# Gated networks: a fourth room for raw up weights, the fourth block's parts in an unread quarter of x

## Chip, cores and metric

The kernel runs on one core of a Trainium2 chip. A core has five engines that work side by side and wait for each other through semaphores: PE (TensorE: matmuls; PEld is its weight load), DVE (VectorE), ACT (ScalarE), POOL (GpSimd) and SP (SyncE, which here only issues DMAs). The metric is the device time of one execution in microseconds.

## The reference

Two residual layers over 512 tokens with 1024 channels. The first mixes tokens by a grouped state-space model, the second by attention with forget gates; each is followed by a gated network, which is what this change is about.

```python
def conv_ffn(h, w_up, conv_w, conv_b, w_down):
    up = h @ w_up                      # 1024 -> 2 * 2816
    a, b = jnp.split(up, 2, axis=-1)
    ...                                # a_conv: causal depthwise conv (width 3) of a
    return (jax.nn.silu(a_conv) * b) @ w_down

for i in range(DEPTH):                 # DEPTH = 2
    shift, scale, gate = adaln_params(c, ada_w[i, 0], ada_b[i, 0])
    hn = modulate(h, norm_g[i, 0], shift, scale)
    m = s5_mixer(...) if i % 2 == 0 else fox_mixer(...)
    h = h + gate * m
    shift, scale, gate = adaln_params(c, ada_w[i, 1], ada_b[i, 1])
    hn = modulate(h, norm_g[i, 1], shift, scale)
    h = h + gate * conv_ffn(hn, ffn_w_up[i], ffn_conv_w[i], ffn_conv_b[i], ffn_w_down[i])
return rmsnorm(h, final_g)
```

## The kernel before

Everything is float32. For PE a value is split into two rounded parts, `hi` (ACT, L303) and `lo` = value - `hi` (DVE, L304), by `put_parts`; a product of two such values is three matmuls, `hi*hi`, `hi*lo` and `lo*hi`. Activations lie with channels on the 128 partitions and tokens in the free dimension. The normed input of a gated network is `x`, a pair of tiles `a_hi` and `a_lo`, each of 8 blocks of 128 channels by 512 tokens.

**Pairs.** The 44 output blocks of `w_up` come as 22 pairs, f = 0 to 21: block 2f belongs to `a` of the reference, block 2f + 1 to `b`. A block is 128 rows by 1024 inputs, loaded as one raw tile of 512 KB. Pairs 0 to 3 of each layer are computed plainly (`product`, L320, 24 matmuls of 512 columns for a block). Pairs 4 to 21 go through `quarters`, which takes the two blocks of a pair, cut in two along the inputs, and `x`, cut in two along inputs and along tokens, as 2 by 2 block matrices, and forms their product from seven block products (L588) instead of eight. Each of the seven is 12 matmuls of 256 columns. Four kinds of weights are made for a pair:

- `a11`, `a12`: the two halves of the first block `a`, rounded as they are (1024 columns);
- `s1`, `s2` (tile c) and `s4`, `s3` (tile d): sums of quarters, four DVE instructions of L556 (`sums`), and then rounded (2 x 1024 columns);
- `a22`: the second half of the second block `b`, rounded as it is (512 columns).

On the other side stand quarters of `x` and four sums of quarters, `t1` to `t4`, which `forms_x` makes once a layer, during the plain pairs. The seven products are `a11*b11`, `s1*t1`, `a12*b21`, `s2*t2`, `s4*b22`, `a22*t4`, `s3*t3`. They read the quarters b11, b21 and b22 of `x` (first inputs and first tokens, second inputs and first tokens, second inputs and second tokens); none reads the fourth quarter, b12 (first four blocks of channels, tokens 256 to 511). ACT copies some products out of PSUM (L595, `nm_h`), DVE adds them up (L556, `nm_t`), and `gated` does the convolution (L638, L640), the gate (L643, L650) and the rounding of the result `g` (`ghi`, `glo`). Between pairs the blocks of the down product of the group before (`w_down`, L320, result added to `h` at L402) are computed.

**Rooms.** A raw block stays in its room until ACT and DVE have read it. The tag `raw` has three rooms (`RAW` in the second line quoted below), through which nearly all raw weights go in turn: the two blocks of each pair, and in the second layer also the pieces of `w_down`, which in the first layer have two rooms of their own (`rawd`, L194). The raw blocks of a pair are both loaded with `self.raw` at the head of `quarters`. SP issues these loads in the order in which the program has them and waits, at each, until the room is free. The rounded parts of `a22` have one room of their own in the network's pool, `w_hi` of 640 and `w_lo` of 544 columns; those of all others come from five rooms each.

**Order.** A scheduler at build time puts each engine's instructions in a fixed order, by its own estimate of when each would be ready; at run time an engine takes them strictly in that order. In the first layer DVE has additional work up to pair 16: 24 reductions (`ada_units`, L273) that make the modulation of the next layers, on blocks that POOL loads into the single room `ada_raw`.

Of the kernel before, what the change touches and what calls it, by code (L numbers as in the profile page):

```python
# [9 lines left out]
F32 = mybir.dt.float32  # L10
F32R = mybir.dt.float32r
# [7 lines left out]
P = 128  # L19
D = 1024  # L20
KT = D // P
# [46 lines left out]
ROOM, ASIDE, VALUES = 9 * P, 22, 16  # L68
# [7 lines left out]
def part_of(pool, shape, name, tag, bufs, aside=0):  # L76

    _, n, w = shape
    t = pool.tile([P, ROOM if bufs == WB else n * w + P], F32R, name=name, tag=tag, bufs=bufs)
    return t[:, aside:aside + n * w].rearrange("p (n w) -> p n w", w=w)  # L80


class Trunk:
# [464 lines left out]
    def quarters(self, pool, l, f, x, finish):  # L548

        nc = self.nc  # L550
        H, N = KT // 2, S // 2
        t1, t2 = HALVES
        a, b = (self.raw([P, KT, P], self.io["w_up"][l][2 * f + j]) for j in range(2))
        a11, a12, a21, a22 = a[:, :H], a[:, H:], b[:, :H], b[:, H:]
        c, d = (pool.tile([P, 2, H, P], F32, name="sums", bufs=2) for _ in range(2))
        sub = lambda o, u, v, op=ALU.subtract: nc.vector.tensor_tensor(o, u, v, op)  # L556
        w = {}
        copied = self.copied

        def parts(src, names, *where):  # L560
            hi, lo = (
                pool.tile([P, H * P + (P if n == "w_hi" else 32)], F32R, name=n, tag="e" + n)[:, ASIDE:ASIDE + H * P].rearrange("p (n w) -> p n w", w=P)
                if where else part_of(self.wpool, [P, len(names) * H, P], n, n, WB, ASIDE)
                for n in ("w_hi", "w_lo")
            )
            with self.behind(*copied):
                self.put_parts(hi, lo, src)
            for j, n in enumerate(names):
                w[n] = hi[:, j * H:(j + 1) * H], lo[:, j * H:(j + 1) * H]

        parts(a, ("a11", "a12"))
        sub(c[:, 0], a21, a22, ALU.add)
        sub(c[:, 1], c[:, 0], a11)
        parts(c.rearrange("p n k m -> p (n k) m"), ("s1", "s2"))
        sub(d[:, 1], a11, a21)
        sub(d[:, 0], a12, c[:, 1])
        parts(d.rearrange("p n k m -> p (n k) m"), ("s4", "s3"))
        parts(a22, ("a22",), pool)
        quarter = lambda k, t: tuple(v[:, k * H:(k + 1) * H, t] for v in x)
        xs = {"b11": quarter(0, t1), "b21": quarter(1, t1), "b22": quarter(1, t2)}  # L580
        for n, v in self.tx.items():
            xs[f"t{n}"] = v

        def times(o, wn, xn, first=True):
            (whi, wlo), (xhi, xlo) = w[wn], xs[xn]
            for k in range(H):
                for n, (wt, xt) in enumerate(((whi, xhi), (whi, xlo), (wlo, xhi))):
                    self.last_mm = nc.tensor.matmul(  # L588
                        o, wt[:, k], xt[:, k], start=(first and k == 0 and n == 0), stop=(k == H - 1 and n == 2),
                        skip_group_check=True,  # L590
                    )

        def copy(o, last=False):
            t = self.tmp.tile([P, N], F32, name="nm_h", bufs=4)
            a = nc.scalar.activation(t, o, AF.Copy)  # L595
            if last:
                self.copied = [a.ins]
            return t

        p1, p5 = (self.mm.tile([P, S], F32, name="mmp")[:, :N] for _ in range(2))  # L600
        p2, p4 = (self.aux.tile([P, S], F32, name="aux")[:, :N] for _ in range(2))
        oa, ob = (self.tmp.tile([P, S], F32, name="nm_t") for _ in range(2))
        times(p1, "a11", "b11")
        c1 = copy(p1)
        times(p5, "s1", "t1")
        c5 = copy(p5)
        times(p2, "a12", "b21")
        sub(oa[:, t1], p2, c1, ALU.add)
        times(p1, "s2", "t2", False)
        c2 = copy(p1, True)  # L610
        times(p5, "s4", "b22", False)
        sub(oa[:, t2], p5, c2, ALU.add)
        finish(2 * f, oa, slice(0, S))
        times(p4, "a22", "t4")
        c4 = copy(p4)
        times(p1, "s3", "t3", False)
        sub(ob[:, t2], p1, c5, ALU.add)
        sub(ob[:, t1], p1, c4)
        finish(2 * f + 1, ob, slice(0, S))
# [98 lines left out]
class Ew:  # L718
# [29 lines left out]
    def sub(self, a, b, out=None):  # L748
        return self.tt(a, b, ALU.subtract, out)
# [1147 lines left out]
```

## Time and profile before

| | |
|---|---|
| timed runs, median of 3 | 1200.07 us (1199.22 to 1203.46) |
| profiled execution | 1197.47 us, span of its trace 1195.7 us |
| mean granted clock of PE | 0.996 |
| bytes read from HBM, and their rate | 173.73 MB, 151 GB/s over the span |
| plain pairs and pair products of the first layer | up to 565 us; first pair product at 296.35 us |
| pair products of the second layer | 890 to 1149 us |
| SP waiting to load raw blocks until DVE has rounded a block (L304) | 468.4 us in 128 waits |
| SP waiting for the same until DVE has formed sums (L556) | 166.0 us in 18 waits |

How to read the rows below. A row of the page's first part gives an engine's busy time, its share of the span and its instructions. In the view by stages each row is a stretch of time (microseconds from the span's start) with its length, the busy time of each engine, the granted clock of PE and what the DMA engines did. A row of waits reads: engine, what it was to write, its line, `<-` who released it: total, number, longest. A row in order of time has the start, the duration, the engine, the line, the operation, `out<-in`, the shape, and in brackets how long the engine had been idle and what ended that. A row with `min/median/max` gives the durations in nanoseconds of all instructions of one kind.

### The profile page before, as it was taken

Reading aid. Unit: us, or ns where it says so; the run is one execution under the profiler, and the core shown is the slowest. Engines: PE = TensorE matmul, PEld = TensorE weight load, DVE = VectorE, ACT = ScalarE, POOL = GpSimd, SP = SyncE. Lnnn points to the kernel's source line nnn. Section 1 sums busy time; section 2 is a strip of 40 time slices with the busy share of each in tenths; the row PEclk is TensorE's granted clock in tenths of the full one; section 3 lists DMA queues with packets and bytes.
Section 4 is the critical chain, followed back from the end, with each engine's and each line's share of the span. In section 5 each row is a group of like instructions: output and inputs, shape, how many; then the busy total and the mean of one; then the engine's idle time right before and its main releaser. Section 6 shows DMA issues by size and latency. Waiting matters only on the chain.

```text
span 1195.7 us, 20776 instructions
## 1 busy us (share of the span) xinstructions
PE 1174.6 (98%) x7983; PEld 1021.7 (85%) x7983; DVE 1011.1 (85%) x1836; ACT 619.9 (52%) x1186; POOL 124.1 (10%) x230
## 2 busy tenths in 40 slices
PE   9999999999999899999999999999999999999997
PEld 4566678898999889999998788878989999999987
DVE  8989887889999989998786678867899887888865
ACT  3564644436554445455452566564456555545543
POOL 3231012100000000000000444330000000000000
PEclk9999999999999999999999999999999999999999
DMA  9588777721554445332454444433122342323331
GB/s 371 202 330 275 214 249 274 271 73 53 177 176 133 168 167 185 133 102 87 151 175 165 139 150 157 139 111 106 56 88 80 124 136 76 110 90 110 111 101 72
DMA packets 72115, 182.02 MB, mean 152 GB/s; under 512 B 23135, under 2 KB 25023, under 8 KB 70991
## 3 DMA queue, kind: packets, MB, share of 16 engines
q1 hardware_dynamic: 58767, 136.77, 34.5%
q0 software_dynamic: 11920, 43.26, 10.1%
q8 instruction: 63, 1.03, 0.3%
q10 hardware_dynamic: 1328, 0.66, 0.2%
q14 instruction: 37, 0.30, 0.1%
HBM read 173.73 MB, written 6.92 MB: 151 GB/s over the span
## 4 chain that ended last, share of the span: by engine, by line
PE 58%; issue 19%; DVE 12%; DMA 7%; ACT 1%; POOL 1%; SPq 0%; DVEq 0%; POOLq 0%; ACTq 0%
PE mmp L320 24%; PE mmp L588 12%; PE aux L588 5%; PE mmp L1277 4%; DVE w_lo L304 3%; DMA raw<-in_w_up 3%; PE mmp L1617 2%; PE aux L1035 1%; PE aux L1756 1%; PE mmp L229 1%; DVE sums L556 1%; PE aux L1776 1%; PE aux L1147 1%; DVE h L402 1%; DVE conv L640 1%
## 5 line engine op out<-in xcount | busy, mean ns | idle before, releaser
L304 DVE TENSOR_TENSOR w_lo<-raw,w_hi 128x1024 fp32r<-128x1024 f32 (+4 forms) x173 | 181.0, 1050 | 29.8 <-ACT w_hi L303 29.4
L303 ACT ACTIVATE w_hi<-raw 128x1024 fp32r<-128x1024 f32 (+4 forms) x173 | 154.0, 898 | 97.3 <-PE mmp L320 40.2
L320 PE MATMUL mmp<-ghi,w_hi 128*128 128x512 f32 (+1 forms) x412 | 147.5, 358 | 0.0
L320 PE MATMUL mmp<-glo,w_hi 128*128 128x512 f32 (+1 forms) x412 | 147.3, 358 | 0.0
L320 PE MATMUL mmp<-ghi,w_lo 128*128 128x512 f32 (+1 forms) x412 | 146.8, 356 | 0.0
L588 PE MATMUL mmp<-w_hi,w_lo 128*128 128x256 f32 x432 | 120.1, 278 | 3.3 <-DVE w_lo L304 3.3
L588 PE MATMUL mmp<-w_hi 128*128 128x256 f32 x432 | 120.1, 278 | 1.0 <-ACT nm_h L595 1.0
L588 PE MATMUL mmp<-w_lo,w_hi 128*128 128x256 f32 x432 | 119.7, 277 | 0.0
L320 PE MATMUL mmp<-a_hi,w_hi 128*128 128x512 f32 (+1 forms) x304 | 109.7, 364 | 0.0
L320 PE MATMUL mmp<-a_hi,w_lo 128*128 128x512 f32 (+1 forms) x304 | 107.9, 355 | 0.0
L320 PE MATMUL mmp<-a_lo,w_hi 128*128 128x512 f32 (+1 forms) x304 | 107.8, 356 | 0.0
L303 ACT ACTIVATE w_hi<-sums 128x1024 fp32r<-128x1024 f32 x80 | 83.9, 1058 | 44.3 <-DVE sums L556 38.9
L304 DVE TENSOR_TENSOR w_lo<-sums,w_hi 128x1024 fp32r<-128x1024 f32 x80 | 97.6, 1219 | 0.6 <-ACT w_hi L303 0.6
L595 ACT ACTIVATE nm_h<-mmp 128x256 f32<-128x256 f32 x108 | 40.3, 379 | 100.8 <-PE mmp L588 100.5
L320 PEld LDWEIGHTS mmp<-ghi,w_lo 128*128 128x128 f32 x412 | 77.4, 188 | 11.7
L320 PEld LDWEIGHTS mmp<-ghi,w_hi 128*128 128x128 f32 x412 | 77.3, 188 | 10.6
L320 PEld LDWEIGHTS mmp<-glo,w_hi 128*128 128x128 f32 x412 | 77.4, 188 | 10.2
L588 PEld LDWEIGHTS mmp<-w_hi,w_lo 128*128 128x128 f32 x432 | 81.5, 189 | 3.7 <-DVE w_lo L304 3.7
L588 PEld LDWEIGHTS mmp<-w_hi 128*128 128x128 f32 x432 | 81.7, 189 | 1.5 <-ACT nm_h L595 1.4
L588 PEld LDWEIGHTS mmp<-w_lo,w_hi 128*128 128x128 f32 x432 | 81.6, 189 | 0.0
L588 PE MATMUL mmp<-a_hi,w_lo 128*128 128x256 f32 x288 | 80.1, 278 | 0.8 <-DVE w_lo L304 0.8
L588 PE MATMUL mmp<-a_hi,w_hi 128*128 128x256 f32 x288 | 80.2, 278 | 0.6 <-ACT w_hi L303 0.6
(337 smaller groups left out, 3138.7 us busy)
## 6 DMA issues: line engine op xcount, KB each, us to landing
raw<-in_w_up SPq DMA_DIRECT2D x88, 512.0 KB, 3.7
ada_raw<-in_ada_t POOLq DMA_DIRECT2D x40, 512.0 KB, 4.1
raw<-in_ada_w POOLq DMA_DIRECT2D x24, 512.0 KB, 7.2
nf<-nfd SPq DMA_DIRECT2D x8, 1152.0 KB, 7.8
raw<-in_ada_w SPq DMA_DIRECT2D x16, 512.0 KB, 10.0
raw<-in_fox_qk SPq DMA_DIRECT2D x16, 512.0 KB, 3.6
raw<-in_w_down SPq DMA_DIRECT2D x24, 320.0 KB, 2.9
rawd<-in_w_down SPq DMA_DIRECT2D x24, 256.0 KB, 3.9
```

What stands on the lines that cost most here:

```text
L229: self.last_mm = nc.tensor.matmul(ps[32 * qq:32 * qq + 32, :], self.sc32[:, k, :], w[:, q * S:(q + 1) * S], start=(step is steps[0]), stop ...
L303: self.rounded = nc.scalar.activation(hi, src, AF.Copy).ins
L304: return nc.vector.tensor_tensor(lo, src, hi.bitcast(F32), ALU.subtract)
L320: self.last_mm = self.nc.tensor.matmul(o if len(xt.shape) == 2 else by_place(o), wt, xt, start=(k == 0 and n == 0), stop=(k == nk - 1 and ...
L402: add = self.nc.vector.scalar_tensor_tensor(h, ps, self.par[i][:, 16 + m:17 + m], h, op0=ALU.mult, op1=ALU.add,)
L556: sub = lambda o, u, v, op=ALU.subtract: nc.vector.tensor_tensor(o, u, v, op)
L588: self.last_mm = nc.tensor.matmul(o, wt[:, k], xt[:, k], start=(first and k == 0 and n == 0), stop=(k == H - 1 and n == 2), skip_group_che ...
L595: a = nc.scalar.activation(t, o, AF.Copy)
L640: c = nc.vector.scalar_tensor_tensor(t[:, d:], ps[:, :S - d], cw[:, 2 - d, f:f + 1], t[:, d:], op0=ALU.mult, op1=ALU.add)
L1035: nc.tensor.matmul(ps[:, :, cols], x[:, q, r].rearrange("p c j -> p (c j)"), both[:, :, planes, q, :], start=(r == 0), stop=(r == 1), skip ...
L1277: one = lambda k: nc.tensor.matmul(ps, w[m][:, k, :], x[:, k], start=(k == 0), stop=(k == KT - 1))
L1617: self.last_mm = nc.tensor.matmul(ps[q, b][:, :n], xt[:, k, tb], wt, start=(k == 0 and i == 0), stop=(k == KT - 1 and i == 2),)
```

## The change

Two things. The second block of a pair with an odd f is loaded into a new tile, `rawx`, with one room in the network's pool; a pair with an even f loads both blocks through `raw` as before. And the rounded parts of `a22` no longer have a room of their own: they are written into the quarter b12 of `a_hi` and `a_lo`, four runs of 128 columns, each in the second half of one of the first four blocks of channels. The old room held 640 + 544 columns of 4 bytes; `rawx` holds 1024.

```diff
-        a, b = (self.raw([P, KT, P], self.io["w_up"][l][2 * f + j]) for j in range(2))
+        a = self.raw([P, KT, P], self.io["w_up"][l][2 * f])
+        if f % 2:
+            b = pool.tile([P, KT, P], F32, name="rawx", bufs=1)
+            nc.sync.dma_start(b, self.io["w_up"][l][2 * f + 1])
+        else:
+            b = self.raw([P, KT, P], self.io["w_up"][l][2 * f + 1])
...
-        def parts(src, names, *where):
+        def parts(src, names, where=None):
             hi, lo = (
-                pool.tile([P, H * P + (P if n == "w_hi" else 32)], F32R, name=n, tag="e" + n)[:, ASIDE:ASIDE + H * P].rearrange("p (n w) -> p n w", w=P)
+                where[i][:, :H, N + ASIDE:N + ASIDE + P]
                 if where else part_of(self.wpool, [P, len(names) * H, P], n, n, WB, ASIDE)
-                for n in ("w_hi", "w_lo")
+                for i, n in enumerate(("w_hi", "w_lo"))
             )
...
-        parts(a22, ("a22",), pool)
+        parts(a22, ("a22",), x)
```

Lines behind the edit count five higher in the changed kernel: L556 becomes L561, L588 becomes L593. Only the pair products' surroundings are put in another order; POOL's order is the same, and of PE's matmuls 159 change places, all in pairs 10 to 14 of the first layer.

On SP, the first layer's loads from the last plain pairs to pair 9, before:

```order
L194 DMA rawd<-in_w_down 128x512 x2
L197 DMA raw<-in_w_up 128x1024 x7
L194 DMA rawd<-in_w_down 128x512 x2
L197 DMA raw<-in_w_up 128x1024 x2
L194 DMA rawd<-in_w_down 128x512 x2
```

And now, in the same place:

```order
L194 DMA rawd<-in_w_down 128x512 x2
L556 DMA rawx<-in_w_up 128x1024
L197 DMA raw<-in_w_up 128x1024 x7
L194 DMA rawd<-in_w_down 128x512 x2
L197 DMA raw<-in_w_up 128x1024
L556 DMA rawx<-in_w_up 128x1024
L194 DMA rawd<-in_w_down 128x512 x2
```

Pair 5's second block now stands ahead of all loads that wait for a room of `raw`, and each odd pair's is a load of its own.

On DVE, from the convolution of pair 12 to the rounding of pair 13's tile c (`w_lo<-sums`, the weights of `s1` and `s2`), before:

```order
L650 TENSOR_TENSOR conv<-conv,nm_t 128x512
L280 TENSOR_TENSOR par_94<-ada_s,rest 128x8
L402 SCALAR_TENSOR_TENSOR h<-mmp,par_93,h 128x512
L282 SCALAR_TENSOR_TENSOR ga_98<-par_94,rest 128x8
L304 TENSOR_TENSOR glo<-conv,ghi 128x512
L402 SCALAR_TENSOR_TENSOR h<-mmp,par_93,h 128x512
L304 TENSOR_TENSOR w_lo<-sums,w_hi 128x1024
L273 ISA ada_raw,ada_s<-ada_raw,c_row 128x1024
```

And now:

```order
L280 TENSOR_TENSOR par_94<-ada_s,rest 128x8
L402 SCALAR_TENSOR_TENSOR h<-mmp,par_93,h 128x512
L282 SCALAR_TENSOR_TENSOR ga_98<-par_94,rest 128x8
L655 TENSOR_TENSOR conv<-conv,nm_t 128x512
L304 TENSOR_TENSOR w_lo<-sums,w_hi 128x1024
L304 TENSOR_TENSOR glo<-conv,ghi 128x512
L402 SCALAR_TENSOR_TENSOR h<-mmp,par_93,h 128x512
L273 ISA ada_raw,ada_s<-ada_raw,c_row 128x1024
```

The rounding of `s1` and `s2` has moved ahead of `glo` and of the second `h`.

On DVE once more, around the last rounding of pair 14 (tile d, `w_lo<-sums` behind `sums<-sums,raw` of pair 15), before:

```order
L556 TENSOR_TENSOR sums<-raw,sums 128x512
L556 TENSOR_TENSOR sums<-raw 128x512
L556 TENSOR_TENSOR nm_t<-aux,nm_h 128x256
L556 TENSOR_TENSOR sums<-sums,raw 128x512
L304 TENSOR_TENSOR w_lo<-sums,w_hi 128x1024
```

And now:

```order
L561 TENSOR_TENSOR sums<-raw,sums 128x512
L304 TENSOR_TENSOR a_lo<-raw,a_hi 128x4x128
L561 TENSOR_TENSOR sums<-rawx 128x512
L561 TENSOR_TENSOR sums<-sums,raw 128x512
L304 TENSOR_TENSOR w_lo<-sums,w_hi 128x1024
L561 TENSOR_TENSOR nm_t<-aux,nm_h 128x256
```

The rounding of `a22` (now `a_lo`, four runs of 128) comes directly ahead of it instead of earlier, and the adding of a product, `nm_t`, behind it.

## The prediction

> **What bounds the kernel now.** I read the page first, then the busy time by stages, then who waited for whom inside the two stretches of pair products, and last single rows in order of time.
>
> ```profile
> PE 1174.6 (98%) x7983; PEld 1021.7 (85%) x7983; DVE 1011.1 (85%) x1836; ACT 619.9 (52%) x1186; POOL 124.1 (10%) x230
> ```
>
> PE is busy nearly throughout, so only its few holes can be won. The view by stages (pairs 4 to 9 of the first layer, its pairs 10 to 14, the rest of that layer, all pairs of the second layer) shows where they are:
>
> ```profile
> core 0: us, PE busy (x) PEld busy (x) DVE busy (x) ACT busy (x) POOL busy (x), PEclk, DMA share, GB/s
> 296.00:383.00 87.00, 87.00 (x637) 81.76 (x636) 85.00 (x137) 47.18 (x77) 5.31 (x10) 1.00 0.48 161
> 383.00:462.00 79.00, 73.45 (x518) 68.36 (x517) 73.82 (x116) 39.25 (x63) 4.79 (x9) 0.98 0.47 167
> 462.00:565.00 103.00, 103.00 (x749) 96.66 (x748) 93.70 (x147) 53.95 (x88) 2.12 (x4) 1.00 0.38 121
> 890.00:1149.00 259.00, 258.03 (x1886) 242.27 (x1885) 219.08 (x329) 138.85 (x220) 0.00 (x0) 1.00 0.35 109
> ```
>
> Up to 383 us DVE has no free time left (85.00 of 87.00 us) while PE is still ahead of what it needs. From 383 to 462 us the reserve is used up: PE is idle for 79.00 - 73.45 = 5.55 us and has a mean clock of 0.98. After that it has no hole, and in the whole second layer 259.00 - 258.03 = 0.97 us. The waits of the first layer from 296 to 462 us name both sides:
>
> ```profile
> PE mmp L588 <- DVE w_lo L304: 4.1, 4, 2.0
> PE aux L588 <- DVE w_lo L304: 0.9, 1, 0.9
> PE mmp L588 <- ACT w_hi L303: 0.6, 1, 0.6
> DVE sums L556 <- DMA raw<-in_w_up: 3.6, 2, 2.0
> ```
>
> PE waits for weights that DVE has yet to round (4.1 + 0.9 + 0.6 = 5.6 us, the whole loss), and DVE, which is the limit here, itself stands still twice for a raw block that has not landed. These rows in order of time show the mechanism:
>
> ```profile
> 388.81 0.33 SPq L197 DMA_DIRECT2D raw<-in_w_up  x1
> 393.28 0.69 DVE L556 TENSOR_TENSOR sums<-raw 128x512 f32<-128x512 f32 x1 [1.58 <-DMA raw<-in_w_up]
> 418.63 0.33 SPq L197 DMA_DIRECT2D raw<-in_w_up  x1
> 424.98 0.69 DVE L556 TENSOR_TENSOR sums<-raw 128x512 f32<-128x512 f32 x1 [1.99 <-DMA raw<-in_w_up]
> 430.98 0.28 PE L588 MATMUL mmp<-a_hi,w_hi 128*128 128x256 f32 x1
> 435.52 0.38 PE L588 MATMUL mmp<-w_hi,w_lo 128*128 128x256 f32 x1 [1.99 <-DVE w_lo L304]
> 438.88 0.42 DVE L556 TENSOR_TENSOR nm_t<-aux,nm_h 128x256 f32<-128x256 f32 x1 [0.93 <-PE aux L588]
> 456.66 1.22 DVE L304 TENSOR_TENSOR w_lo<-sums,w_hi 128x1024 fp32r<-128x1024 f32 x1
> 457.93 0.39 PE L588 MATMUL mmp<-a_hi,w_lo 128*128 128x256 f32 x1 [0.18 <-DVE w_lo L304]
> ```
>
> The second block of pair 11 can be asked for only at 388.81, when a room of the three comes free, and DVE wants it at 393.28 - 1.58 = 391.70, 2.9 us later; pair 13's is asked for at 418.63. After the longest hole, which ends at 435.52, PE also runs at half its clock:
>
> ```profile
> 435.90:439.30 3.40, 3.40 (x19) 3.40 (x18) 2.47 (x6) 1.55 (x3) 0.53 (x1) 0.50 0.30 100
> ```
>
> 3.40 us at 0.50 lose another 1.7 us. PE has thus lost 5.55 + 1.7 = 7.25 us by the end of pair 14, and that is the most the first layer can give back.
>
> **The loads.** The number of transfers stays the same, and those that now go to `rawx` are issued by the same queue. With four rooms the block that a room is loaded with is used two pairs after the one that left it. Pair 11's second block follows pair 9's, so it can be asked for about one pair (15 us) earlier than at 388.81; pair 13's follows pair 11's. A load takes 3.7 us (its row stands below), so both waits of DVE go: **1.58 + 1.99 = 3.57 us**. No row shows a fourth room; the bounds are nothing gained, and all of it.
>
> ```profile
> raw<-in_w_up SPq DMA_DIRECT2D x88, 512.0 KB, 3.7
> ```
>
> **From DVE to PE.** The last rounding for which PE waits is the one at 456.66, in pair 14. Counted along both orders from pair 9, exactly the same DVE work stands ahead of it; only places within have changed. Its time therefore moves by DVE's idle time alone. Besides the two waits that is the 0.93 us at 438.88, where DVE waited for the third product of pair 13. In the changed order DVE gets there at 438.88 - 0.93 - 3.57 = 434.4. Pair 13 started at 430.98 and will start at least the 1.58 us of the first wait earlier, at 429.4; its first 36 matmuls at 0.11 us each (starts at 435.75 and 435.86 below) end at about 433.4, and the rounding that held them, formerly begun at 434.26, comes before `glo` and one `h` in the new order (0.60 + 0.66 us, the steps between their starts) and so begins at 434.26 - 1.26 - 3.57 = 429.4. PE is there first, and I count the 0.93 as gone: bounds 0 and 0.93. Sum for DVE: 4.50 us.
>
> ```profile
> 432.99 0.68 DVE L304 TENSOR_TENSOR glo<-conv,ghi 128x512 fp32r<-128x512 f32 x1
> 433.60 0.74 DVE L402 SCALAR_TENSOR_TENSOR h<-mmp,par,h 128x512 f32<-128x512 f32 x1
> 434.26 1.21 DVE L304 TENSOR_TENSOR w_lo<-sums,w_hi 128x1024 fp32r<-128x1024 f32 x1
> 435.75 0.28 PE L588 MATMUL mmp<-w_hi 128*128 128x256 f32 x1
> 435.86 0.35 PE L588 MATMUL mmp<-w_lo,w_hi 128*128 128x256 f32 x1
> ```
>
> PE gains less than that. Behind this rounding the order of pair 14 now leaves 33 matmuls to run where it left 28, since fewer of `a22` are put ahead: 5 x 0.11 = 0.55 us. **First layer: 4.50 - 0.55 = 3.95 us.** This leaves 7.25 - 3.95 = 3.3 us of PE's losses: the holes of pairs 10 and 12 stay, those of 11 and 13 close, and pair 14's grows from 0.18 to about 1.4 us, because DVE is still the limit. From pair 15 on nothing is late next: DVE had time to spare there (93.70 of 103.00 us).
>
> **Second layer.** DVE is not the limit (219.08 of 259.00 us), and most of its waits for raw blocks cost PE nothing:
>
> ```profile
> DVE sums L556 <- DMA raw<-in_w_up: 25.9, 13, 3.6
> PE mmp L588 <- ACT nm_h L595: 1.0, 2, 0.5
> 1053.41 1.29 DVE L556 TENSOR_TENSOR sums<-raw 128x512 f32<-128x512 f32 x2 [1.82 <-DMA raw<-in_w_up]
> 1062.39 0.63 ACT L303 ACTIVATE ghi<-conv 128x512 fp32r<-128x512 f32 x1 [1.08 <-DVE conv L650]
> 1063.35 0.38 PE L588 MATMUL mmp<-w_hi 128*128 128x256 f32 x1 [0.45 <-ACT nm_h L595]
> 1069.38 0.69 DVE L556 TENSOR_TENSOR sums<-raw 128x512 f32<-128x512 f32 x1 [3.35 <-DMA raw<-in_w_up]
> 1080.53 0.39 PE L588 MATMUL mmp<-w_hi 128*128 128x256 f32 x1 [0.52 <-ACT nm_h L595]
> ```
>
> 25.9 us of waits over 18 pairs, and two holes of PE, 0.45 and 0.52 us. Both follow a wait for raw: DVE is late, ACT stands at `ghi` for `conv`, and the copy of a product that PE needs is queued behind it. Pairs 16 and 17 read these blocks; 16's room now comes free one use sooner and 17's second block is in `rawx`. I take both holes as closed, each with the slower restart (0.38 instead of 0.28): 0.97 + 0.2 = **1.2 us**; bounds 0 and 1.2.
>
> **The moved rounding.** 36 ACT and 36 DVE instructions write four runs of 128 columns instead of one of 512. No row has this very form; the nearest are a read of four such runs and writes in runs of 128:
>
> ```profile
> L526 DVE TENSOR_TENSOR x<-a_hi,a_lo x8: 1216/1218/1219, 266.0 to 863.1; 128x1024 f32<-128x1024 f32 x8
> L304 DVE TENSOR_TENSOR plo<-aux,phi x48: 412/619/692, 670.2 to 811.2; 128x512 fp32r<-128x512 f32 x24, 128x384 fp32r<-128x384 f32 x16, 128x256 fp32r<-128x256 f32 x8
> L304 DVE TENSOR_TENSOR glo<-conv,ghi x44: 677/684/693, 277.8 to 1152.7; 128x512 fp32r<-128x512 f32 x44
> ```
>
> At most 692 ns in runs against 684 ns in one piece: I take 0; with the ends, 11 pairs (4 to 14) x 8 ns = 0.1 us. The new wait, pair 4's rounding behind the last read of that quarter by pair 3's plain product, has behind it on ACT a rounding which itself waited for DVE until 293.81; the read it waits for is the twelfth of pair 3's last 24 matmuls (0.23 us each by the two starts below), which ends at about 296.35 - 12 x 0.23 = 293.6, so it costs at most half a us on ACT, and PE reaches those weights only after 296.35 + 12 x 0.11 us. I take 0. Its end is that half us, in each layer.
>
> ```profile
> 293.81 1.06 ACT L303 ACTIVATE w_hi<-sums 128x1024 fp32r<-128x1024 f32 x1 [1.92 <-DVE sums L556]
> 430.52 0.39 PE L320 MATMUL mmp<-glo,w_hi 128*128 128x512 f32 x1
> 430.75 0.39 PE L320 MATMUL mmp<-ghi,w_lo 128*128 128x512 f32 x1
> 296.35 0.28 PE L588 MATMUL mmp<-a_hi,w_hi 128*128 128x256 f32 x1
> ```
>
> **The sum.** 3.95 + 1.2 = 5.15 us off the profiled execution of 1197.47 us (span 1195.7): 1192.3. The three timed runs have their median at 1200.07, 2.6 us above that execution, so I forecast **1194.9 us**. Half a per cent, about what a measurement of this kernel can tell from no change, is 6.0 us, or 1194.07; the forecast lies just inside it.
>
> **Rivals.**
> Better order (A): the changed order also closes the holes of pairs 10, 12 and 14. For it speaks that DVE now forms the sums of the next pair earlier; against it that DVE stays full. All of PE's losses, 7.25 + 1.2 = 8.45 us: 1191.6.
> The clock (B): the slow stretch is not tied to the hole and comes again in the changed kernel, now under DVE's limit, so that DVE waits for PE as before: 0.93 us less, 1195.8. For it speaks that the holes of 1.29 us (pair 11) and 0.86 us (pair 12) drew no half clock; against it that the only one of 1.99 us did.
> The Trainium skill's page "TensorE: Matmul & The Clock Gate" (Part 1, "What's actually happening") states that the array falls to half clock after an idle window of about 3.4 us and watches free-running windows. By that rule a hole of 1.99 us alone should not do it, which is this rival's 1195.8; the trace differs on what sets it off and agrees on the length, 3.40 us.
> Hidden anyway (C): the waits go but DVE meets others in their place (a result of PE, the single `ada_raw` room), or the holes only move to pairs 12 and 14. Gain 0 to 2 us: 1198 to 1200. For it speaks that this rounding of `a22` and all of DVE's work remain.
> Slower (D): writing into `x` in runs is dearer on DVE. Place: pairs 4 to 14, where DVE is the limit; it decides from 5.15 / 11 = 0.47 us per rounding. At three times the price (11 x 2 x 0.68 = 15 us) the time is 1200.07 + 15 - 5.15 = 1209.9; against it stand the rows above.
>
> **How the numbers follow.** Forecast 0.47, A 0.20, B 0.10, C 0.19, D 0.04. The forecast with its bounds (the 0.93 in or out, the 1.2 in or out, and some of A) lies at 1192.5 to 1197.0. The range takes in most of A and of C: 1190.0 to 1200.0, leaving out about 0.2. Faster by over 0.5%: A and some two fifths of the forecast, 0.39; slower by over 0.5%: D alone, 0.04; the rest within it, 0.57.
>
> **What would show it.** Right: in the first layer no DVE wait for `raw` or `rawx`; in 296 to 462 us PE's idle time down from 5.55 to about 3 us, no hole in pairs 11 and 13, a longer one in pair 14, no 0.50 clock; in the second layer the 25.9 us of waits about halved and the two holes behind `nm_h` gone; the roundings into `a_lo` at 0.68 us. Wrong: roundings over 0.75 us; new waits of DVE on PE or `ada_raw` of several us; holes in the second layer; PE holes in pairs 5 to 9.

## The result and the profile after

The changed kernel took 1191.12 us (median of 5 runs, 1189.39 to 1193.33), the kernel before, on the same chip, 1200.07 us (median of 5, 1198.33 to 1203.46): ratio 0.9918, 95% interval 0.9894 to 0.9942. The profiled execution of the changed kernel took 1191.44 us (span 1189.6 us). The forecast of 1194.9 us was 3.8 us too high, with its sign right: it lay just inside half a per cent, the result lies outside; a second set of runs (e5) gave 1193.93 us, 0.9945 (0.9925 to 0.9964). The two intervals overlap at 0.9925 to 0.9942, a gain of about 7 to 9 us.

The first row of the changed kernel's page, busy time and share of the span by engine:

```profile
PE 1172.0 (99%) x7983; PEld 1019.0 (86%) x7983; DVE 1012.6 (85%) x1836; ACT 618.9 (52%) x1186; POOL 123.4 (10%) x230
```

PE's busy time fell by 2.6 us (1174.6 before), DVE's work stayed. The view by stages of the changed kernel, same stretches and columns as in the prediction:

```profile
296.00:383.00 87.00, 87.00 (x636) 81.78 (x635) 85.78 (x137) 47.21 (x78) 5.29 (x10) 1.00 0.49 161
383.00:462.00 79.00, 77.47 (x546) 71.84 (x545) 78.95 (x127) 40.77 (x66) 5.31 (x10) 1.00 0.51 175
462.00:565.00 103.00, 103.00 (x749) 96.65 (x748) 92.71 (x145) 56.36 (x92) 1.59 (x3) 1.00 0.37 115
890.00:1149.00 259.00, 259.00 (x1882) 243.09 (x1881) 220.68 (x332) 139.35 (x222) 0.00 (x0) 1.00 0.35 108
```

From 383 to 462 us PE's idle time went from 5.55 to 1.53 us, the clock from 0.98 to 1.00, and DVE's idle time from 5.18 to 0.05 us: DVE now works without a pause and is still the limit. The waits of the changed kernel from 296 to 462 us (who, what, line, released by: total, number, longest):

```profile
PE mmp L593 <- DVE w_lo L304: 1.3, 2, 0.8
DVE ada_raw L273 <- DMA ada_raw<-in_ada_t: 1.0, 2, 0.6
PE mmp L593 <- ACT w_hi L303: 0.2, 1, 0.2
```

No wait of DVE for `raw` or `rawx` is left. Rows in order of time show why, and what remains of PE's holes (the rows at 388.74 and 417.68 are the next loads through the three rooms of `raw`):

```profile
373.75 0.33 SPq L556 DMA_DIRECT2D rawx<-in_w_up  x1
388.74 0.93 SPq L197 DMA_DIRECT2D raw<-in_w_up  x2
389.19 0.69 DVE L561 TENSOR_TENSOR sums<-rawx 128x512 f32<-128x512 f32 x1
389.82 0.38 PE L593 MATMUL mmp<-a_hi,w_hi 128*128 128x256 f32 x1 [0.19 <-ACT w_hi L303]
391.08 0.38 PE L593 MATMUL mmp<-a_hi,w_lo 128*128 128x256 f32 x1 [0.76 <-DVE w_lo L304]
401.44 0.33 SPq L556 DMA_DIRECT2D rawx<-in_w_up  x1
417.07 0.39 PE L593 MATMUL mmp<-w_hi,w_lo 128*128 128x256 f32 x1 [0.58 <-DVE w_lo L304]
417.68 0.93 SPq L197 DMA_DIRECT2D raw<-in_w_up  x2
418.47 0.69 DVE L561 TENSOR_TENSOR sums<-rawx 128x512 f32<-128x512 f32 x1
450.10 1.22 DVE L304 TENSOR_TENSOR w_lo<-sums,w_hi 128x1024 fp32r<-128x1024 f32 x1
451.24 0.42 DVE L561 TENSOR_TENSOR nm_t<-aux,nm_h 128x256 f32<-128x256 f32 x1
```

Pair 11's second block is asked for at 373.75 and first read at 389.19; pair 13's at 401.44 and 418.47. Before, each had 2.9 and 4.4 us between the request and the moment when DVE wanted it, now 15.4 and 17.0 us.

Two layers and the attention between them can be timed from the first matmul of pair 4 and of pair 21 in each layer. In the kernel before (the start of its pair 4 stands in the prediction, 296.35):

```profile
555.39 0.28 PE L588 MATMUL mmp<-a_hi,w_hi 128*128 128x256 f32 x1
890.03 0.28 PE L588 MATMUL mmp<-a_hi,w_hi 128*128 128x256 f32 x1
1139.32 0.28 PE L588 MATMUL mmp<-a_hi,w_hi 128*128 128x256 f32 x1
```

and in the changed kernel:

```profile
296.69 0.28 PE L593 MATMUL mmp<-a_hi,w_hi 128*128 128x256 f32 x1
549.40 0.28 PE L593 MATMUL mmp<-a_hi,w_hi 128*128 128x256 f32 x1
886.33 0.28 PE L593 MATMUL mmp<-a_hi,w_hi 128*128 128x256 f32 x1
1133.19 0.28 PE L593 MATMUL mmp<-a_hi,w_hi 128*128 128x256 f32 x1
```

So the first layer takes 549.40 - 296.69 = 252.71 us instead of 259.04, the second 246.86 instead of 249.29, and the stage between them 336.93 instead of 334.64. The first two are 6.33 and 2.43 us less; the attention, whose order had not been touched, took 2.29 us more. Whether that is the change's doing, and whether 6.33 us is its usual gain, one pair of profiles cannot say. The same three times, read in the same way from every profile of this study, answer it (us; "room" is the fourth room, by layer):

| profile | room | first layer | attention | second layer |
|---|---|---|---|---|
| before | none | 259.04 | 334.64 | 249.29 |
| e1, before again | none | 257.86 | 336.24 | 249.59 |
| e2, rounding in x alone | none | 257.29 | 339.20 | 250.15 |
| e3 | first | 253.73 | 337.51 | 248.61 |
| e4 | second | 257.69 | 337.33 | 246.86 |
| the change | both | 252.71 | 336.93 | 246.86 |
| e5, the change again | both | 254.83 | 339.15 | 246.86 |
| e6, before, short reductions | none | 249.67 | 335.50 | 248.40 |
| e7, the change, short reductions | both | 249.67 | 336.53 | 246.86 |
| e8, the change, slower pace | both | 250.53 | 336.77 | 246.86 |
| e9, before, slower pace | none | 250.03 | 337.33 | 251.09 |
| e10, room held late | both, late | 257.47 | 336.42 | 246.86 |
| e11, as e8 | both | 250.57 | 337.21 | 246.86 |

### The profile page after: what moved, and what is told of

It is laid out like the page before. It is cut to its first block, busy times and chain, and to the rows that moved or that the text cites. A ratio compares the mean times of both kernels' runs of the same rounds, so it can differ in the third digit from the quotient of the medians.

```text
span 1189.6 us, 20776 instructions
## 1 busy us (share of the span) xinstructions
PE 1172.0 (99%) x7983; PEld 1019.0 (86%) x7983; DVE 1012.6 (85%) x1836; ACT 618.9 (52%) x1186; POOL 123.4 (10%) x230
## 5 line engine op out<-in xcount | busy, mean ns | idle before, releaser
L304 DVE TENSOR_TENSOR w_lo<-raw,w_hi 128x1024 fp32r<-128x1024 f32 (+3 forms) x137 | 160.1, 1173 | 41.4 <-ACT w_hi L303 41.0
L303 ACT ACTIVATE w_hi<-raw 128x1024 fp32r<-128x1024 f32 (+3 forms) x137 | 132.2, 969 | 83.5 <-PE mmp L320 45.2
L593 PE MATMUL mmp<-w_hi,w_lo 128*128 128x256 f32 x432 | 119.3, 277 | 0.6 <-DVE w_lo L304 0.6
L593 PE MATMUL mmp<-w_hi 128*128 128x256 f32 x432 | 119.3, 276 | 0.0
L593 PE MATMUL mmp<-w_lo,w_hi 128*128 128x256 f32 x432 | 119.3, 276 | 0.0
L593 PEld LDWEIGHTS mmp<-w_hi,w_lo 128*128 128x128 f32 x432 | 81.0, 188 | 0.8 <-DVE w_lo L304 0.8
L593 PEld LDWEIGHTS mmp<-w_lo,w_hi 128*128 128x128 f32 x432 | 81.1, 188 | 0.0
L593 PEld LDWEIGHTS mmp<-w_hi 128*128 128x128 f32 x432 | 81.1, 188 | 0.0
L593 PE MATMUL mmp<-a_hi,w_lo 128*128 128x256 f32 x288 | 80.0, 278 | 0.8 <-DVE w_lo L304 0.8
L402 DVE SCALAR_TENSOR_TENSOR h<-mmp,par,h 128x512 f32<-128x512 f32 (+1 forms) x104 | 69.0, 667 | 13.4 <-PE mmp L320 13.1
```

The source lines that it names most:

```text
L303: self.rounded = nc.scalar.activation(hi, src, AF.Copy).ins
L304: return nc.vector.tensor_tensor(lo, src, hi.bitcast(F32), ALU.subtract)
L402: add = self.nc.vector.scalar_tensor_tensor(h, ps, self.par[i][:, 16 + m:17 + m], h, op0=ALU.mult, op1=ALU.add,)
L593: self.last_mm = nc.tensor.matmul(o, wt[:, k], xt[:, k], start=(first and k == 0 and n == 0), stop=(k == H - 1 and n == 2), skip_group_che ...
```

## The experiments

Every time is a median; each ratio is to the kernel before, run beside it, whose median lay between 1199.81 and 1200.35 us.

**e1: the kernel before, once more.**

> The kernel before, once more. Theory V (part of the 8.95 us comes from how the kernel before varies from run to run): the half-clock stretch and the holes of the first layer are not the same in each execution; from pair 4 to pair 21 of the first layer this profile differs from 259.04 us by over 1 us, or the attention stage between the two gated networks differs from 334.65 us by over 1 us. Theory L (the raw blocks that land late set the first layer): both repeat within 0.5 us, and what differs between timed runs lies elsewhere. Time: ratio 1.000, within 0.2%.

Measured: 1199.49 us, ratio 0.9992 (0.9980 to 1.0005). The first layer took 257.86 us, 1.18 less than in the first profile, and the attention 1.59 more. V holds: the first layer of one and the same kernel differs by over a microsecond. The wait for pair 11's block repeats (2.03 us), that for pair 13's does not: that block is read at 424.43 without a wait, and in e2 and e4, which also have three rooms there, DVE hardly waits for it either (none in e2, 0.13 us in e4). Instead there is a short wait for pair 14's second block, at 442.90:

```profile
394.65 0.69 DVE L556 TENSOR_TENSOR sums<-raw 128x512 f32<-128x512 f32 x1 [2.03 <-DMA raw<-in_w_up]
424.43 1.29 DVE L556 TENSOR_TENSOR sums<-raw 128x512 f32<-128x512 f32 x2
442.90 1.29 DVE L556 TENSOR_TENSOR sums<-raw 128x512 f32<-128x512 f32 x2 [0.67 <-DMA raw<-in_w_up]
```

**e2: the rounding's place alone, three rooms.** Of the changed kernel only the loads are as before:

```diff
-        a = self.raw([P, KT, P], self.io["w_up"][l][2 * f])
-        if f % 2:
-            b = pool.tile([P, KT, P], F32, name="rawx", bufs=1)
-            nc.sync.dma_start(b, self.io["w_up"][l][2 * f + 1])
-        else:
-            b = self.raw([P, KT, P], self.io["w_up"][l][2 * f + 1])
+        a, b = (self.raw([P, KT, P], self.io["w_up"][l][2 * f + j]) for j in range(2))
```

> Only the fourth block's rounding goes into the normed x; every raw block still goes round three rooms. Theory L (the room counts, because raw blocks land earlier): the first layer from pair 4 to pair 21 stays at 259.0 us within 0.7, the second at 249.3 within 0.5, DVE still waits for raw about as often, and the time stays within 0.15% of the kernel before (1198 to 1202 us). Theory O (the new order of instructions, or the rounding's new place, gains by itself): the first layer falls to 253 us or the second to 247, and the time to 1195 us or less.

Measured: 1199.93 us, 0.9997 (0.9986 to 1.0009); first layer 257.29 us, second 250.15 us. This is L, though the first layer is 1.7 us below the 259.0 that was expected, and near e1's 257.86. The rounding is in `x` and the memory of its old room is free: neither gains anything that can be measured. The other half of O, the new order, is not tried by this: the traces show that DVE and PE run both gated networks of e2 in the order of the kernel before, names of tiles aside, and no run has the changed kernel's order without its room. The rows of the changed kernel speak against the order as a gain by itself: it reads pair 11's second block at 389.19 and pair 13's at 418.47, while the three rooms of `raw` take their next block only at 388.74 and 417.68. With a load of 3.7 us, a block asked for there would come some 3 us after DVE wants it, each time (an estimate from these rows). The moved rounding takes as long as ever, as the view of the tile `a_lo` in e2 has it (least, median and longest duration in ns):

```profile
L304 DVE TENSOR_TENSOR a_lo<-raw,a_hi x36: 678/687/695, 297.9 to 1140.0; 128x512 fp32r<-128x512 f32 x36
```

And DVE's waits for raw in e2's second layer (view of waits, 884 to 1143 us) are as before (25.9 us in 13):

```profile
DVE sums L556 <- DMA raw<-in_w_up: 27.8, 14, 4.1
```

**e3 and e4: the room in one layer only.**

```diff
-        if f % 2:
+        if f % 2 and l == 0:
...
-        if f % 2:
+        if f % 2 and l == 1:
```

> The fourth room in the first gated network alone; in the second one the rounding still goes into the normed x, with three rooms. Theory L: from pair 4 to pair 21 the first layer is 252.7 us within 0.7 (259.0 before), the second stays at 249.3 within 0.5; the time is 6 us less than before, 1192 to 1196 us. Theory O: the second layer falls to about 247 us without the room as well. Theory A (the attention stage's 2.3 us more belong to the changed kernel): that stage is near 336.9 us here too; if it is chance, it is anywhere between 334.5 and 337.

> The fourth room in the second gated network alone; in the first one the rounding still goes into the normed x, with three rooms. Theory L: the first layer stays at 259.0 us within 0.7, the second falls to 246.9 within 0.3; the time is 2.4 us less than before, 1196 to 1199 us. Theory O: the first layer falls to about 253 us without the room as well, and the time to 1193 us or less.

Measured: e3 1195.21 us, 0.9965 (0.9952 to 0.9979), with a first layer of 253.73 us and a second of 248.61; e4 1196.75 us, 0.9972 (0.9961 to 0.9983), with 257.69 and 246.86 us. Each layer gains where its room is and nowhere else, and the two ratios multiply to 0.9937, between the two results of the whole change. e3's two layers and e4's first miss what was expected of them by 0.2 to 0.6 us; the expectations rested on the first pair of profiles alone. Of O, the rounding's place gains in neither; the order changed only where the room was. The attention took 337.5 and 337.3 us, and 339.2 us in e2, which has no fourth room at all: its 2.3 us more in the changed kernel's profile are chance, and the 334.64 us of the profile before are the shortest of all thirteen.

**e5: the changed kernel, once more.**

> The changed kernel once more, for a second profile and more timed runs. Theory L: the first layer from pair 4 to pair 21 is again 252.7 to 253.7 us (257.3 to 259.0 in the four profiles without the room there), the second 246.9 (248.6 to 250.2 without); the attention stage is somewhere from 334.7 to 339.2, as in the others, since it is chance; the ratio is 0.993 within 0.0015 (4.8 and 2.5 us of 1200, with 1 us for fewer half-clock stretches). If the first result's 0.9918 stands, something gains 2 us beside the two layers' raw loads.

Measured: 1193.93 us, 0.9945 (0.9925 to 0.9964), at the end of what was expected. The second layer is again 246.86 us, the first 254.83, 2.1 us more than in the first profile. Most of that is a half-clock stretch (3.41 us at 0.50, so 1.7 us), which came here in the changed kernel too, after two holes of pair 10. PE's rows in order of time in e5:

```profile
390.67 0.38 PE L593 MATMUL mmp<-a_hi,w_hi 128*128 128x256 f32 x1 [0.91 <-ACT w_hi L303]
391.93 0.39 PE L593 MATMUL mmp<-a_hi,w_lo 128*128 128x256 f32 x1 [0.76 <-DVE w_lo L304]
```

And the stretch that follows, in the view by stages of e5:

```profile
392.82:396.23 3.41, 3.41 (x18) 3.41 (x17) 3.41 (x5) 1.13 (x2) 0.00 (x0) 0.50 0.84 336
```

**e6 and e7: DVE relieved, without and with the change.** Both compute the attention's modulation from 64 of each row's 1024 columns:

```diff
             sums = self.sums[i, t]
+            n_ada = 64 if i == 2 else D
...
-                    w, w, self.c_row, 1.0, 0.0, ALU.mult, ALU.add, sums[:, j:j + 1]
+                    w[:, :n_ada], w[:, :n_ada], self.c_row[:, :n_ada], 1.0, 0.0, ALU.mult, ALU.add, sums[:, j:j + 1]
```

> The kernel before with the reductions of the first gated network's ada rows cut from 1024 to 64 columns (the modulation of the attention stage then comes from a sixteenth of its weights; loads, instructions and all else stay). Theory D (late raw blocks cost the first layer because DVE has no time to spare there): DVE's 24 reductions of 1.1 us become some 0.2 us each, DVE gets ahead again after a wait, and the first layer from pair 4 to pair 21 falls from 258 us to 254 or less, though raw still lands as late. Rival P (a late block stops TensorE directly, however free DVE is): the first layer stays at 257 us or more.

> The changed kernel with the same reductions cut to 64 columns. Theory D: the first layer is within 1.5 us of that of the kernel before with the cut (so the room's 4.8 us there shrink to under 1.5), at 251.5 to 252.5 us; the second layer keeps its 2.5 us; the two cut kernels' times differ by 2.5 to 4.5 us. Rival P: the first layers differ by 4 us or more still, the times by 7 or more.

Measured: e6 1190.84 us, 0.9915 (0.9894 to 0.9936); e7 1187.59 us, 0.9894 (0.9871 to 0.9916); they differ by 3.25 us. The first layer is 249.67 us in both, to the hundredth, below the 251.5 that was expected. The second layer accounts for 1.54 us of the difference (248.40 and 246.86), less than the 2.5 expected; the rest is not located. The stretch from 383 to 462 us in the view by stages, first of e6:

```profile
383.00:462.00 79.00, 79.00 (x572) 74.03 (x571) 71.30 (x131) 41.99 (x68) 5.83 (x11) 1.00 0.58 179
```

and of e7:

```profile
383.00:462.00 79.00, 79.00 (x574) 74.10 (x573) 71.39 (x132) 42.26 (x68) 5.83 (x11) 1.00 0.59 179
```

PE has no hole, DVE 7.7 us to spare, with three rooms as with four. So 249.67 us is what the first layer takes when nothing but PE limits it, and there the room's gain of 4 us is gone altogether: D, not P. One part of the expectation was wrong: raw does not land late in e6. Between 296 and 565 us e6 has no wait of DVE for it, since it is DVE itself that gives the rooms back, and in e6 it does so in time: pair 11's second block is asked for at 377.42, 11.4 us before the 388.81 of the kernel before. A late block in the first layer was a consequence of DVE's lateness before it was a cause.

**e8 and e11: the reductions at a slower pace, with the change; e9: the same with three rooms.**

```diff
                         self.room = None
-                        self.tick(ticks)
+                        if j % 2:
+                            self.tick(ticks)
```

> The changed kernel with every second of the ada reductions that follow a pair's down products left to later pairs (three for two pairs in place of four). Theory D: DVE has half a microsecond more in each of pairs 4 to 16, the remaining holes of TensorE in pairs 10 and 12 (2.0 us in the changed kernel) close, and the time falls 1 to 2 us below the changed kernel's, to 1189.5 to 1190.5. Rival: the reductions that come later take the slack of pairs 17 to 21 and open holes there, or the holes are set by loads and not by DVE's load; then the time stays within 0.7 us of the changed kernel's or goes above it.

> The changed kernel with the slower pace once more, beside other kernels: the first layer 250.5 us within 0.7, the second 246.9, TensorE without a hole over 0.3 us from pair 4 to pair 21 of the first layer, and the time 1187.5 to 1190.5 us, below both kernels.

> The kernel before (three rooms, the fourth block's rounding in tiles of its own) with the slower pace of the ada reductions alone. Theory D (the room pays in the first layer only because DVE is full there): the pace alone brings the first layer from pair 4 to pair 21 from 258 us to 252 or less, within 1.5 us of the 250.5 that it has with the room, and raw waits of DVE there all but go; the second layer stays at 248.4 to 250.2; the time is 1193 to 1196 us, and the room is then worth 2.5 to 5 us on top (1188.1 with both). Rival S (room and pace are two separate gains): the first layer stays some 4 us above the 250.5 us of both, at 254 or more, and the time is 1195.5 or more.

Measured: with the change 1188.14 us, 0.9897 (0.9875 to 0.9918), and again 1188.99 us, 0.9907 (0.9883 to 0.9931); with three rooms 1192.69 us, 0.9935 (0.9911 to 0.9959). The stretch from 383 to 462 us in the view by stages, first of e8:

```profile
383.00:462.00 79.00, 78.93 (x569) 73.62 (x568) 77.24 (x122) 42.55 (x70) 3.76 (x8) 1.00 0.55 171
```

and of e9:

```profile
383.00:462.00 79.00, 79.00 (x565) 73.75 (x565) 77.73 (x123) 42.61 (x69) 4.23 (x8) 1.00 0.53 169
```

In e9's second layer the waits for raw (view of waits, 884 to 1143 us) are as many as before:

```profile
DVE sums L556 <- DMA raw<-in_w_up: 29.9, 13, 4.9
```

All of the reductions are still done, only spread over more pairs, and PE's holes all but close (within 0.9 us of the 249.67 of e6 and e7): the first layer takes 250.5 us with the room and 250.0 without, 8 us less than before. D again, and S fell: once DVE has time, the room is worth nothing in the first layer. What it adds to the slower pace is in the second layer, 251.09 - 246.86 = 4.2 us in this pair of profiles; e9's 251.09 is the longest of the six second layers with three rooms and 0.9 us above what was expected, and against their mean of 249.52 it is 2.7 us. e9's time lies 0.3 us below the range expected. e8 was expected at 1 to 2 us below the changed kernel and came out 5.8 us below e5: the estimate had counted the holes of one profile, whose first layer was the best of three. The version with both is the fastest that computes everything.

**e10: the room held late.** The block of `rawx` is kept until the next even pair's tile d is formed:

```diff
             nc.sync.dma_start(b, self.io["w_up"][l][2 * f + 1])
+            self.held = l, b
...
         sub(d[:, 0], a12, c[:, 1])
+        if f % 2 == 0 and f > 4:
+            assert self.held[0] == l
+            one = pool.tile([P, 1], F32, name="one", bufs=1)
+            sub(one, self.held[1][:, 0, :1], d[:, 0, 0, :1])
```

> The changed kernel, but the fourth room stays held until the next even pair's d is formed (one more subtraction of a single column, which reads the held block and d): an odd pair's second block then starts to load as late as with three rooms. Theory L (the earlier load is what the room gives): the first layer goes back to 257 to 259 us and the second to 248.4 to 250.2, the time to 1198 to 1201 us. Rival M (the room pays because the ring of three no longer has to serve four blocks, so that the other three of two pairs come earlier): most of the gain stays, the first layer under 255, the second under 247.5, the time 1192 to 1196 us.

Measured: 1196.73 us, 0.9977 (0.9962 to 0.9992). Here the theories share the result between them. The first layer went back to 257.47 us, which is L; the second stayed at 246.86 us, which is M. The rows of e10 in order of time show the first layer's wait come back: the holding instruction, the request behind it, and the wait, which was 1.58 us before.

```profile
388.41 0.16 DVE L562 TENSOR_TENSOR one<-rawx,sums 128x1 f32<-128x1 f32 x1
388.60 0.33 SPq L556 DMA_DIRECT2D rawx<-in_w_up  x1
394.13 0.69 DVE L562 TENSOR_TENSOR sums<-rawx 128x512 f32<-128x512 f32 x1 [1.81 <-DMA rawx<-in_w_up]
```

So the first layer speaks for L. One thing besides the late block differs there: e10's edit also gave DVE an order that is neither of the other two. The five instructions `one` up to pair 14 take 0.16 us each, 0.8 us at most of the 3.7 us that the first layer lost against the mean of 253.8 with the room.

The second layer of e10 hardly has any wait (view of waits, 884 to 1143 us):

```profile
DVE sums L562 <- DMA raw<-in_w_up: 3.9, 4, 1.8
DVE sums L562 <- DMA rawx<-in_w_up: 2.0, 2, 1.1
```

25.9 us of waits shrink to 5.9. But the experiment does not part L from M in this layer, since the block in the fourth room does not come as late here as with three rooms. Pair 17's second block is asked for at these times, first before the change, then in the changed kernel, then in e10:

```profile
1065.02 0.33 SPq L197 DMA_DIRECT2D raw<-in_w_up  x1
1042.91 0.33 SPq L556 DMA_DIRECT2D rawx<-in_w_up  x1
1050.48 0.33 SPq L556 DMA_DIRECT2D rawx<-in_w_up  x1
```

Pair 17 starts on PE at 1075.75, 1070.44 and 1073.77, so the request stands 10.7, 27.5 and 23.3 us ahead of it: e10 took back only a part of the earlier request. What M says can be seen as well. Pair 16's second block, which goes through the ring of three in all of these kernels, is asked for 8.7 us ahead of its pair before (1049.98, pair at 1058.63) and 17.7 us ahead in the changed kernel (1036.43, pair at 1054.08), since a quarter of the up blocks no longer go through the ring, which here serves the pieces of `w_down` too. How the second layer's gain divides between the two stays open. In the first layer, where `w_down` has rooms of its own, e10's block is as late as before (388.60 and 388.81), and the gain went with the early request.

## Why the prediction came out as it did

**The raw waits (3.57 us): right, but the size was in part luck.** Both are gone, in e3 and e5 too, and pair 11's block is asked for at 373.75, 15.1 us before the 388.81 of the kernel before, where one pair (15 us) was forecast. e10 speaks for the earlier load as the cause. The 1.99 us for pair 13's block belonged to that one execution: DVE could read it only 6.35 us after the request (418.63 to 424.98), where the median of these loads is 3.7 us. In e1, e2 and e4 it is not late, and the waits for raw in the same stretch, 296 to 462 us, are 2.7, 1.8 and 2.0 us.

**DVE's other wait (0.93 us): right; "exactly the same DVE work stands ahead": wrong by 0.33 us.** One instruction, `nm_t<-aux`, now follows the last rounding of pair 14 (451.24 behind 450.10), which the rows of the order showed and the count missed. That rounding came 6.90 us earlier against the start of pair 4 (153.41 us after it instead of 160.31), where 4.50 was forecast. Of the difference, 0.33 is this instruction; 0.78 is idle time of DVE that also went before 383 us (2.00 to 1.22 us) and 0.63 small idle times after it (5.13 us went there, 4.50 were counted). The rest, some 0.7 us, no run took apart; an instruction of 0.69 us starts 0.60 us after its predecessor when it need not wait, so each wait that goes may save 0.09 us beyond its idle time.

**Fewer matmuls behind that rounding (-0.55 us), pair 14's hole growing to 1.4 us: wrong.** With DVE another 2.4 us earlier, it did not open: pair 14 has no hole over 0.25 us. The holes of pairs 10 and 12 stayed and those of 11 and 13 closed, as forecast.

**First layer 3.95 us: right in size, by two errors that cancel.** In the first pair of profiles it is 6.33 us, but the mean of the four profiles with three rooms and all of DVE's work (259.04, 257.86, 257.29, 257.69) is 257.97 us, of the three with the room (252.71, 254.83, 253.73) it is 253.76: 4.2 us. The profile of before was 1.1 us above its own kind: its 1.99 us wait for pair 13's block comes in none of the other three, its half-clock stretch in e2 alone. Against that, the terms left out some of what went (the 0.78 and 0.63 us of DVE's idle time above) and took off 0.55 us that pair 14 did not lose.

**Second layer 1.2 us: this is the step that failed.** It is 2.43 us in the first pair and 2.7 in the mean (249.52 us in six profiles with three rooms, 248.40 to 251.09; 246.86 in all seven with four). The term was read off PE's idle time of 0.97 us, and this view leaves out a part of each hole. A matmul is shown as 0.28 us long while the next follows after 0.11; a start that is late by less than about 0.17 us is not idle time, and a longer hole shows with as much missing. These rows are from pair 6 of the second layer before the change:

```profile
914.31 0.28 PE L588 MATMUL mmp<-w_lo,w_hi 128*128 128x256 f32 x1
914.42 0.28 PE L588 MATMUL mmp<-w_hi,w_lo 128*128 128x256 f32 x1
914.68 0.38 PE L588 MATMUL mmp<-a_hi,w_hi 128*128 128x256 f32 x1
914.91 0.28 PE L588 MATMUL mmp<-a_lo,w_hi 128*128 128x256 f32 x1
915.16 0.38 PE L588 MATMUL mmp<-a_hi,w_lo 128*128 128x256 f32 x1
915.38 0.28 PE L588 MATMUL mmp<-a_hi,w_hi 128*128 128x256 f32 x1
```

From 914.42 to 915.38 four steps take 0.96 us where they should take 0.45, and no row shows idle time. From the starts of pairs, pairs 6 and 14 lost 0.61 and 0.24 us in this hidden way, pairs 16 and 17 0.75 and 0.82: 2.42 us, which is what the layer gained. The mechanism (DVE late by a raw block, PE behind it) was right. That pair 16's room comes free sooner and that pair 17's block is in `rawx` both fit the requests shown under e10; how much each does was not measured. The waits for raw there went from 25.9 us in 13 to less than the half that was forecast:

```profile
DVE sums L561 <- DMA raw<-in_w_up: 7.3, 5, 3.2
```

**The moved rounding at no cost: right.** In the changed kernel (least, median, longest in ns):

```profile
L304 DVE TENSOR_TENSOR a_lo<-raw,a_hi x18: 685/690/702, 298.2 to 1115.2; 128x512 fp32r<-128x512 f32 x18
L304 DVE TENSOR_TENSOR a_lo<-rawx,a_hi x18: 684/688/707, 313.9 to 1125.1; 128x512 fp32r<-128x512 f32 x18
```

**The rivals.** A came nearest in time (1191.6), but not by its mechanism: the holes of pairs 10 and 12 are still there. The changed order was never run without the room, so its share is argued (under e2) and not shown. B's condition did occur, in e5, at the price of a half-clock stretch, but B tied it to a DVE wait that did not come back. C held in none of the three profiles with the room in the first layer; D is excluded by the rows above. From the profiles the change is worth 4.2 + 2.7 = 6.9 us, a ratio of 0.9943, where 5.15 us was forecast. The 2.6 us added for the step from the profiled execution to the median also rested on one draw: that execution had the shortest attention stage of all.

## What to carry to other kernels

Before buying room or time for a transfer that an engine waits for, ask why that engine needs it so soon: here the late blocks of the first layer were asked for late because DVE itself gave the rooms back late, and spreading DVE's side work over more pairs won twice what the room won there (8 us against 4). A hole of PE is measured by the steps between the starts of its matmuls, not by the idle time of a view, which here hides about 0.17 us of each. And one profile is one draw: the same kernel's first layer differed by 1.2 and 2.1 us between two executions, so a term should be checked against a second profile where there is one.

## What the runs showed of the hardware

**The half clock is not tied to one hole's length.** Besides the end of the program, the granted clock fell to 0.50 in three of the thirteen profiles, each time for 3.41 us: in the kernel before from 435.9 us, after a hole of 1.99 us; in e5 from 392.8, after holes of 0.91 and 0.76 us within 1.4 us; and in e2 from 392.1, after like holes of pair 10. In e3 and e4 two holes at the same place drew none, though from start to start they were longer together (2.2 us in each, 2.0 in e5). The Trainium skill, "TensorE: Matmul & The Clock Gate" (Part 1, "What's actually happening"), gives the length as 3413 ns, which agrees, and explains differences between runs by a window that runs free of the program, which would fit that the same holes draw it or not; but that section asks for about 3.4 us of idleness, and no idle time of PE that these thirteen profiles show is longer than 2 us.

**The attention stage varies by itself.** With nothing changed in it, it took 334.64 to 339.20 us over thirteen profiles, and 336.93 and 339.15 us in two of the same kernel. What sets it was not tried; a gain of two or three microseconds in this kernel cannot be read from a span alone, but can from the stages.
